# Dependent steps two k-tiles later, operand sums on VectorE, and another order of the last tokens' norm, in a two-layer decoder kernel

## The chip, the cores and the metric

The kernel runs on one core of a Trainium2 chip. The metric is the device time of one execution in microseconds (us), the median of several. TensorE is called PE, VectorE DVE, ScalarE ACT, GpSimd POOL, SyncE SP. Each engine works through its own queue in order, and waits on semaphores for what other engines produce.

## What is computed

Two decoder layers over 512 tokens of width 1024, all float32 at the interface. Each layer is `h = h + rmsnorm(mixer(rmsnorm(h)))`. Layer 0's mixer (differential attention beside a chunkwise matrix memory, then an output projection) is not touched. Layer 1's mixer, where nearly all of the change lies, is:

```python
def odd_mixer(h, sg_norm_g, w_in, w_spatial, b_spatial, w_out):
    p = jnp.einsum('bsd,de->bse', h, w_in)          # 512 x 1024 by 1024 x 6144
    u, v, z = _split(p, (2048, 2048, 2048))
    u = jax.nn.gelu(u)
    v = rmsnorm(jax.nn.gelu(v), sg_norm_g)
    vg = v.reshape(B, 4, 128, 8, 256)
    wm = w_spatial * causal                         # 8 groups of 128 x 128
    vs = jnp.einsum('gts,bcsgd->bctgd', wm, vg) + b_spatial.T[None, None, :, :, None]
    y = u * vs.reshape(B, S, 2048) * jax.nn.silu(z)
    return jnp.einsum('bse,ed->bsd', y, w_out)      # 512 x 2048 by 2048 x 1024
```

## The kernel before

**Precision.** A float32 matrix product is made from three matmuls: each operand is split into a high half (a rounding copy, on ACT) and a low half (the operand minus its high half, on DVE), and high by high, high by low and low by high are added in PSUM. The names `wh`, `wl` are the halves of weights, `A11s`, `S3s` and the like those of the activations.

**Groups.** Layer 1 is eight groups, 0 to 7. Each multiplies a 512 x 1024 activation block by a 1024 x 1024 weight block with seven half-size products in place of eight. A group is a row of seven phases, P1, P6, P2, P7, Q5, Q4, Q3 (group 0: P1, P2, P7, P6, Q5, Q4, Q3). A phase uses one activation operand (A11, S2, A12, S3, S1, A22, S4 in the usual order) and one weight operand. The S operands are sums of blocks of the activation; `U2` and the reloaded `B` blocks are sums of weight blocks, made partly by DVE (`sum2`) and partly by DMAs that add into their target (`add`, on POOL's queue). Groups 0 and 1 make v, groups 2 to 5 make u and z and multiply them into `y1T`, groups 6 and 7 are the output projection over the two halves of y. Groups 2 to 5 use 256-column matmuls, the others 512-column ones.

**The order of work is written out by hand.** In `Group.run` a phase is eight k-tiles: a k-tile is three matmuls of 512 columns (six of 256). After each k-tile `tick()` advances a counter and issues whatever `later(dt, fn)` has put at that count, so `later(2, f)` puts f's instructions into their engines' queues two k-tiles on. `need(n)` issues the weight splits (`Group.item`) ahead of use: item m holds a quarter of the weights of half a phase. When a half of a bank has its last k-tile (k-tile 6 or 8 of a phase), `hook(ph, q, o)` issues what reads the bank o: copies on ACT and sums on DVE which combine the seven products, and activation functions (`done`). Since queues are in order, an instruction that waits for another engine holds up all that stands behind it in its own queue.

**Hand-over.** The last projection of layer 0 ends with four token tiles (i = 0 to 3). For each, `f1` (L1214) squares the result on ACT (L325), takes the scale `pr` (L1217, DVE, then POOL), `residual` (L1223) adds into h1, `next_norm` squares again and takes `rs_b` (L95, then L96 on POOL), the product `xn_b` (L1203, DVE) follows, PE transposes it (L1136), and `blocks_of` makes the operands A11, A12 (tiles 0, 1) and S3, A22, S2 (tiles 2, 3). `R1`, `R2`, `R3` are k-tile delays in this chain; in the projection a k-tile is also three matmuls of 512 columns. S1 and S4 are sums over all tokens (`sum_split`, L1190).

**Operands of the last projection.** `prepare(c, ph, q, order)` runs during group 5 (c = 0) and group 6 (c = 1). After each phase it splits the operand that takes the slot just freed, in the order A11, A22, A12, S3, S2, S1, S4. The sums that S3, S2 and S1 need (A22 += A21, then A21 += A11, then A11 += A22) are three chained 512 KB DMAs on POOL's queue (L1333 to L1335), issued with the split of A22; the last (A12 = A11 - A12, L1329) is on DVE. The split of S3 is issued five eighths of the way through the group.

**Tail.** In group 7 each output token tile is finished by `value` (squares on ACT, gain on DVE or POOL) and `finish_token`: a sum and a scale on DVE, a power on POOL, two products on DVE (L1455) and two DMAs out. The four finishes stand one after the other in DVE's queue.

Of the kernel before, what the change touches and what calls it, by code (L numbers as in the profile page):

```python
# [41 lines left out]
R2 = (4, 4, 2, 4)  # L42
R3 = (4, 4, 5, 4)
# [13 lines left out]
def hybrid_kernel(tc, x, pre_g0, w_in0, b_ig, b_fg, conv_w, conv_b, lq1, lk1, lq2, lk2,  # L57
# [8 lines left out]
    with ExitStack() as ctx:  # L66
# [912 lines left out]
        def split_block(nm, src, n=0):  # L979

            d = SS[n][nm] = new_split(nm)
            nc.scalar.copy(d[:, 0], src)  # L982
            nc.vector.tensor_tensor(d[:, 1], src, d[:, 0], ALU.subtract)  # L983

        class Group:
# [31 lines left out]
            def item(self, m):  # L1017
# [15 lines left out]

# [13 lines left out]
            def run(self, kind, banks, hook):  # L1047
# [7 lines left out]
                for n, ph in enumerate(self.order):  # L1055
# [5 lines left out]
                    for q, pr in seq:  # L1061
                        need(self.base + 2 * (2 * n + pr + 3 + q) + 2)
# [32 lines left out]
        def combine(g, done):  # L1095

            s1, u2, u3 = new_su(g)

            def hook(ph, q, o):
                if ph == "P1":  # L1100
                    nc.scalar.copy(s1[:, q, :], o)
                elif ph == "P6":
                    if g > 0:
                        nc.vector.tensor_tensor(o, o, s1[:, q, :], ALU.add)
                    nc.scalar.copy(u2[:, q, :], o)
                    if g == 0:
                        b = banks[1][q]
                        nc.vector.tensor_tensor(b, b, u2[:, q, :], ALU.add)
                        nc.scalar.copy(u3[:, q, :], b)
                elif ph == "P2":  # L1110
                    if g == 0:
                        nc.vector.tensor_tensor(o, o, s1[:, q, :], ALU.add)
                    done("C11", q, o)
                elif ph == "P7":
                    if g > 0:
                        nc.scalar.copy(u3[:, q, :], o)
                elif ph == "Q5":
                    nc.vector.tensor_tensor(u3[:, q, :], o, u3[:, q, :], ALU.subtract)
                    done("C22", q, u3[:, q, :])
                elif ph == "Q4":  # L1120
                    done("C21", q, o)
                else:
                    nc.vector.tensor_tensor(u2[:, q, :], o, u2[:, q, :], ALU.subtract)
                    done("C12", q, u2[:, q, :])
            return hook
# [25 lines left out]
        def blocks_of(i, xn):  # L1151
# [14 lines left out]
            low = []  # L1166

            def f0():
                src = turned(i, xn, 0)
                nc.vector.tensor_tensor(s3, Af[0][:, :, t0], src, ALU.subtract)  # L1170
                low.append(split_high("S3", t, s3))

            def f1():
                src = turned(i, xn, 1)
                low.pop()()
                nc.vector.scalar_tensor_tensor(s2, s3, -1.0, src, ALU.mult, ALU.subtract)
                split_tile("A22", t, src)
                low.append(split_high("S2", t, s2))

            def f2():  # L1180
                low.pop()()
                if t == 1:
                    later(6, lambda: sum_split("S1", Af[0][:, :, 0:256], Af[1][:, :, 256:512]))
                    later(16, lambda: sum_split("S4", Af[1][:, :, 0:256], Af[1][:, :, 256:512]))
            later(R3[i], f0)
            later(R3[i] + 1, f1)
            later(R3[i] + 3, f2)

        def sum_split(nm, dst, b):
            nc.vector.tensor_tensor(dst, dst, b, ALU.add)  # L1190
            split_block(nm, dst)
# [22 lines left out]
        def f1(i, o):  # L1214
# [11 lines left out]
            later(R1, residual)  # L1226
# [64 lines left out]
        nc.vector.tensor_reduce(rv, sv, axis=AX.X, op=ALU.add)  # L1291
        rstd_of(rv, rv, 2048, 4)
# [4 lines left out]
        def mix(j, f):  # L1297
# [5 lines left out]
            if f == 0:  # L1303
                y1T.append(slot(YT[j], f"y1T{j}"))
            nc.vector.scalar_tensor_tensor(
                y1T[j][:, f, :].rearrange("p (c t) -> p c t", c=4),
                s[:].rearrange("p (c t) -> p c t", c=4), col(C_SG + 4 * j + f),
                sw["bsp"][:, g, :].unsqueeze(1).to_broadcast([P, 4, P]), ALU.mult, ALU.add)
# [5 lines left out]
        def prepare(c, ph, q, order):  # L1314
# [11 lines left out]

            def step():
                if nm == "S4":
                    nc.vector.tensor_tensor(A12, A11, A12, ALU.subtract)  # L1329
                ST[nm] = tag  # L1330
                split_block(nm, src[nm], c + 1)
                if nm == "A22":
                    nc.gpsimd.dma_start(A22, A21, accum_op=ALU.add)  # L1333
                    nc.gpsimd.dma_start(A21, A11, accum_op=ALU.add)
                    nc.gpsimd.dma_start(A11, A22, accum_op=ALU.add)  # L1335
            later(1, step)

        def uz_group(j):
# [3 lines left out]
            def times(c, q, o, fn):  # L1342
# [9 lines left out]
                if c == "C11":  # L1352
                    later(6 if j == 0 else 1, mul)
                else:
                    mul()

            def done(c, q, o):
# [6 lines left out]
                if c == "C21" and q == 1:  # L1364
                    nc.scalar.preload_act_table(AF.Silu)
                    for q_, o_ in wait:
                        times("C22", q_, o_, AF.Silu)
# [37 lines left out]
        def chunk0():  # L1405
# [3 lines left out]
            def hook(ph, q, o):  # L1409
                if ph == "P1":  # L1410
                    nc.scalar.copy(s1[:, q, :], o)
                elif ph == "P6":
                    nc.vector.tensor_tensor(o, s1[:, q, :], o, ALU.subtract)
                    nc.scalar.copy(u2[:, q, :], o)
# [22 lines left out]
        def chunk1():  # L1437
# [10 lines left out]
            def finish_token(t, q, y0_, y1_):  # L1448
                i = 2 * t + q
                rs = st(1, f"pr1{i}")  # L1450
                nc.vector.tensor_tensor(rs, sq[:, i, 0:1], sq[:, i, 1:2], ALU.add)
                rstd_of(rs, rs, D, 1)
# [71 lines left out]
```

## Time and profile before

| | us |
|---|---|
| time, median of 3 runs | 968.01 (967.96 to 968.61) |
| the profiled execution | 970.75 |
| its span, first to last instruction | 969.0 |
| PE busy in the span | 887.2 |
| DVE, ACT, POOL busy | 577.9, 485.1, 203.6 |
| mean granted PE clock, of full speed | 0.964 |

The span is cut into windows below; a pause of PE inside a window is the window's length less PE's busy time there. A row of a timeline gives in brackets how long the engine stood idle before the instruction and what released it. Ends of matmuls are modelled, so paces are taken from starts.

### The profile page before, as it was taken

The numbers are of one execution on the slowest core, as the hardware profiler recorded it, in microseconds if no ns is written. First come the engines' busy times: TensorE is split into PE (matmuls) and PEld (weight loads), VectorE is DVE, ScalarE is ACT, GpSimd is POOL, SyncE is SP. The second block draws the span as 40 slices with busy tenths as digits, with TensorE's granted clock in tenths as the row PEclk, the third lists the DMA queues.
The fourth block names the chain that finished last, engine by engine and source line by source line (L and its number), as shares of the span: only waits on it lengthen the run. The fifth ranks groups of instructions, "written<-read, shape, count | busy, mean of one in ns | idle before, by whom it ended". The sixth has DMA issues, their size and how long they took to land.

```text
span 969.0 us, 12665 instructions
## 1 busy us (share of the span) xinstructions
PE 887.2 (92%) x4739; PEld 751.6 (78%) x4739; DVE 577.9 (60%) x1026; ACT 485.1 (50%) x926; POOL 203.6 (21%) x276
## 2 busy tenths in 40 slices
PE   7999999999999999999999977998999999386592
PEld 5778888878888888788888755778999999364482
DVE  4467555657754766753431775666767675472675
ACT  5333433446665576654421645675665664352451
POOL 3210022502457135541100210111111011111211
PEclk8999999999999999999999989999999999699797
DMA  8232322312133222222527456676768676559542
GB/s 267 67 131 87 90 63 65 111 43 66 47 89 105 67 66 67 87 87 87 180 103 212 152 135 173 127 221 131 189 147 191 163 182 159 124 110 256 91 108 87
DMA packets 61379, 119.51 MB, mean 123 GB/s; under 512 B 4795, under 2 KB 7942, under 8 KB 61190
## 3 DMA queue, kind: packets, MB, share of 16 engines
q1 hardware_dynamic: 42822, 81.47, 26.1%
q0 software_dynamic: 17344, 34.09, 18.8%
q10 hardware_dynamic: 1152, 3.15, 0.9%
q8 instruction: 37, 0.61, 0.3%
q14 instruction: 24, 0.20, 0.1%
HBM read 111.35 MB, written 4.20 MB: 119 GB/s over the span
## 4 chain that ended last, share of the span: by engine, by line
PE 61%; DVE 13%; ACT 10%; DMA 8%; issue 6%; POOL 1%; SPq 0%; DVEq 0%; POOLq 0%; ACTq 0%
PE pj L275 40%; PE bank L1083 11%; DMA y1T<-y1T 5%; PE bank L1073 2%; PE ao L781 1%; ACT junk L325 1%; PE vs L1301 1%; DMA B<-in_l_w_out_dram 1%; DVE nm L750 1%; DVE U L1013 1%; DMA U<-in_l_w_in_dram 1%; ACT p L751 1%; DVE wlg5P L1024 1%; ACT wh L225 1%; PE sc L745 1%
## 5 line engine op out<-in xcount | busy, mean ns | idle before, releaser
L227 DVE TENSOR_TENSOR wl<-raw,wh 128x512 fp32r<-128x512 f32 x126 | 89.3, 726 | 106.4 <-ACT wh L225 106.0
L275 PE MATMUL pj<-wh,hT 128*128 128x512 f32 x320 | 129.0, 403 | 2.6 <-ACT hT L320 1.3
L275 PE MATMUL pj<-wl,hT 128*128 128x512 f32 x320 | 126.6, 396 | 0.0
L275 PE MATMUL pj<-wh,lT 128*128 128x512 f32 x320 | 126.3, 395 | 0.1
L225 ACT CAST wh<-raw 128x512 fp32r<-128x512 f32 x159 | 93.1, 613 | 40.7 <-DMA raw<-in_l_w_out_dram 19.1
L275 PE MATMUL pj<-hT,wh 128*128 128x512 f32 x192 | 77.8, 405 | 0.2 <-ACT mo L880 0.2
L275 PE MATMUL pj<-hT,wl 128*128 128x512 f32 x192 | 75.8, 395 | 0.0
L275 PE MATMUL pj<-lT,wh 128*128 128x512 f32 x192 | 75.8, 395 | 0.0
L275 PEld LDWEIGHTS pj<-wh,hT 128*128 128x128 f32 x320 | 60.6, 189 | 14.8 <-ACT mz L897 1.7
L275 PEld LDWEIGHTS pj<-wh,lT 128*128 128x128 f32 x320 | 60.5, 189 | 14.1 <-DVE lT L321 0.4
L227 POOL TENSOR_TENSOR wl<-raw,wh 128x512 fp32r<-128x512 f32 x34 | 45.4, 1338 | 119.2 <-ACT wh L225 116.6
L275 PEld LDWEIGHTS pj<-wl,hT 128*128 128x128 f32 x320 | 60.7, 190 | 11.7 <-DVE wl L227 0.4
L751 ACT ACTIVATE p<-sc,nm 128x512 f32<-128x512 f32 (+3 forms) x64 | 33.8, 528 | 47.2 <-DVE nm L750 45.7
L1006 POOL DMA_DIRECT2D B<-in_l_w_in_dram x12 | 15.5, 1292 | 197.9 <-DMA B<-in_l_w_in_dram 54.0
L275 PE MATMUL pj<-wh,yh 128*128 128x512 f32 x128 | 51.2, 400 | 0.0
L275 PE MATMUL pj<-wh,yl 128*128 128x512 f32 x128 | 50.6, 395 | 0.0
L275 PE MATMUL pj<-wl,yh 128*128 128x512 f32 x128 | 50.3, 393 | 0.0
L275 PEld LDWEIGHTS pj<-hT,wl 128*128 128x128 f32 x192 | 36.0, 188 | 8.8
L275 PEld LDWEIGHTS pj<-hT,wh 128*128 128x128 f32 x192 | 36.0, 188 | 8.7 <-ACT mo L880 0.6
L275 PEld LDWEIGHTS pj<-lT,wh 128*128 128x128 f32 x192 | 36.1, 188 | 7.9
L750 DVE TENSOR_REDUCE nm<-sc 128x1 f32<-128x512 f32 (+3 forms) x64 | 31.4, 491 | 2.2
L983 DVE TENSOR_TENSOR S3s<-y1T,S3s 128x1024 fp32r<-128x1024 f32 x2 | 2.5, 1226 | 43.5 <-ACT S3s L982 43.5
(628 smaller groups left out, 2293.3 us busy)
## 6 DMA issues: line engine op xcount, KB each, us to landing
raw<-in_l_w_in_dram SPq DMA_DIRECT2D x64, 512.0 KB, 3.6
B<-in_l_w_in_dram SPq DMA_DIRECT2D x24, 1024.0 KB, 7.7
B<-in_l_w_in_dram POOLq DMA_DIRECT2D x12, 1024.0 KB, 9.2
raw<-in_l_w_out_dram SPq DMA_DIRECT2D x16, 512.0 KB, 4.0
B<-in_l_w_out_dram SPq DMA_DIRECT2D x8, 1024.0 KB, 12.0
U<-in_l_w_in_dram POOLq DMA_DIRECT2D x6, 1024.0 KB, 8.5
B<-in_l_w_out_dram POOLq DMA_DIRECT2D x4, 1024.0 KB, 11.1
y1T<-y1T POOLq DMA_DIRECT2D x6, 512.0 KB, 5.4
```

The lines of the kernel that those rows point to most:

```text
L225: nc.scalar.copy(wh, raw[:, n % 2, :])
L227: eng.tensor_tensor(wl, raw[:, n % 2, :], wh, ALU.subtract)
L275: nc.tensor.matmul(self.outs[i], lhsT=a, rhs=b, start=(n == 0 and m == 0), stop=(n == len(self.ks) - 1 and m == ms[-1]))
L325: nc.scalar.activation(junk[:, :n], src, AF.Square, accum_out=dst)
L745: nc.tensor.matmul(s[:, :n2], lhsT=qs, rhs=dk[p][c][:, h, 0:n2], start=True, stop=False)
L750: nc.vector.reduce_max(nmx[:, c:c + 1], s[:, :nk], axis=AX.X, negate=True)
L751: nc.scalar.activation(pr[:, c, :nk], s[:, :nk], AF.Exp, bias=nmx[:, c:c + 1], accum_out=sm[:, c:c + 1])
L781: nc.tensor.matmul(o[:, i * P:(i + 1) * P], lhsT=aT[:, kb * P:(kb + 1) * P], rhs=dv[p][:, kb, h * P:(h + 1) * P], start=(kb == 0), stop=(k ...
L1006: nc.gpsimd.dma_start(self.X[dst], self.block(nm), accum_op=ALU.add)
L1013: nc.vector.tensor_tensor(at("U2"), at("B11"), at("B12" if self.g else "B22"), ALU.add)
L1073: nc.tensor.matmul(o, lhsT=l, rhs=r, start=(start and k == 0 and m == 0), stop=(k == 3 and m == 2), skip_group_check=True)
L1083: nc.tensor.matmul(o[:, f * 256:(f + 1) * 256], lhsT=l, rhs=r, start=(start and k == 0 and m == 0 and f == 0), stop=(k == 3 and m == 2), s ...
```

## The change

Nearly every step of layer 1 that reads another engine's result is issued two k-tiles after the one that makes it: the low half of a weight pair after its high half, the low half of an operand after its high half, bank copies after bank sums, products after activation functions. The loads and adding DMAs that a freed weight block allows move with the low halves, two k-tiles. The three chained adding DMAs in `prepare` become DVE sums behind the low halves of A22, A12 and S3, and the sum for S4 moves behind the low half of S1. At the hand-over `residual` comes two k-tiles after `f1` instead of three, tile 3's product comes two k-tiles and its operands four k-tiles earlier, tile 2's operands one later; S1 is summed in the same k-tile as tile 3's last operand and is ready some 10 k-tiles earlier. In group 0 the splits for phases three ahead come two k-tiles later. The norm of v moves from the end of group 1 into group 2 (k-tile 4). In the tail the scale and the products of a token tile are issued two k-tiles apart (tokens of the second half) or one (first half), interleaved with the next tile's steps.

```diff
-R2 = (4, 4, 2, 4)
-R3 = (4, 4, 5, 4)
+R2 = (4, 4, 3, 3)
+R3 = (4, 4, 6, 2)
...
-        def split_block(nm, src, n=0):
+        def split_block(nm, src, n=0, then=()):
             d = SS[n][nm] = new_split(nm)
             nc.scalar.copy(d[:, 0], src)
-            nc.vector.tensor_tensor(d[:, 1], src, d[:, 0], ALU.subtract)
+            def low():
+                nc.vector.tensor_tensor(d[:, 1], src, d[:, 0], ALU.subtract)
+                for f in then:
+                    f()
+            later(2, low)
...
                 wh, wl = self.W[ph, pr] = new_pair(f"g{self.g}{ph}{pr}")
-                nc.scalar.copy(wh, src)
-                nc.vector.tensor_tensor(wl, src, wh, ALU.subtract)
-                if ph == "P1" and self.g > 0:
-                    self.sum2(pr)
-                if pr == 0:
-                    return
+                def high():
+                    nc.scalar.copy(wh, src)
+                    later(2, low)
+                def low():
+                    nc.vector.tensor_tensor(wl, src, wh, ALU.subtract)
+                    if ph == "P1" and self.g > 0:
+                        self.sum2(pr)
+                    if pr == 1:
+                        self.freed(ph)
+                if ph == "P6" and self.g == 0:
+                    later(1, high)
+                else:
+                    high()
+            def freed(self, ph):
...
-                        need(self.base + 2 * (2 * n + pr + 3 + q) + 2)
+                        need(self.base + 2 * (2 * n + pr + 3 + (q if self.g or n > 1 else 0)) + 2)
...
-                    if g > 0:
-                        nc.vector.tensor_tensor(o, o, s1[:, q, :], ALU.add)
-                    nc.scalar.copy(u2[:, q, :], o)
-                    if g == 0:
-                        b = banks[1][q]
-                        nc.vector.tensor_tensor(b, b, u2[:, q, :], ALU.add)
-                        nc.scalar.copy(u3[:, q, :], b)
+                elif ph == "P6" and g > 0:
+                    tt(o, o, s1q, ALU.add)
+                    later(2, lambda: copy(u2q, o))
+                elif ph == "P6":
+                    copy(u2q, o)
+                    b = banks[1][q]
+                    later(2, lambda: tt(b, b, u2q, ALU.add))
+                    later(4, lambda: copy(u3q, b))
...
-            later(R3[i], f0)
-            later(R3[i] + 1, f1)
-            later(R3[i] + 3, f2)
+            for n, f in enumerate((f0, f1, f2, f3)):
+                later(R3[i] + 2 * n, f)
...
-            later(R1, residual)
+            later(2, residual)
...
+            then = dict(A22=tt(A22, A22, A21, ALU.add), A12=tt(A21, A21, A11, ALU.add),
+                        S3=tt(A11, A11, A22, ALU.add), S1=tt(A12, A11, A12, ALU.subtract))
             def step():
-                if nm == "S4":
-                    nc.vector.tensor_tensor(A12, A11, A12, ALU.subtract)
                 ST[nm] = tag
-                split_block(nm, src[nm], c + 1)
-                if nm == "A22":
-                    nc.gpsimd.dma_start(A22, A21, accum_op=ALU.add)
-                    nc.gpsimd.dma_start(A21, A11, accum_op=ALU.add)
-                    nc.gpsimd.dma_start(A11, A22, accum_op=ALU.add)
+                split_block(nm, src[nm], c + 1, [then[nm]] if nm in then else ())
             later(1, step)
...
-                if c == "C11":
-                    later(6 if j == 0 else 1, mul)
-                else:
-                    mul()
+                later(2, mul)
...
-            for i in range(4 if j == 0 else 0):
-                v = v1[0][:, i, :]
-                nc.vector.tensor_scalar(v, v, rv[:, i:i + 1], None, ALU.mult)
+            if j == 0:
+                later(4, v_norm)
...
-            def finish_token(t, q, y0_, y1_):
+            def finish_token(t, q, y0_, y1_, dt=2):
...
+                later(dt, norm)
+                later(2 * dt, store)
```

Where a line of a hook is left out above, its DVE sum or ACT copy stays and what reads it moves into `later(2, ...)`.

## Rows read from the trace of the kernel before

**Rows 1.** Page: PE's busy tenths in 40 slices; DMA issues (count, size, us to landing).

```profile
PE   7999999999999999999999977998999999386592
...
B<-in_l_w_out_dram SPq DMA_DIRECT2D x8, 1024.0 KB, 12.0
...
B<-in_l_w_out_dram POOLq DMA_DIRECT2D x4, 1024.0 KB, 11.1
```

**Rows 2.** Windows of the span: us, busy us of each engine (instructions), granted clock, DMA.

```profile
563.00:600.00 37.00, 25.10 (x96) 19.37 (x97) 23.39 (x27) 18.95 (x29) 3.12 (x3) 0.86 0.65 161
600.00:652.80 52.80, 50.33 (x218) 39.95 (x219) 31.73 (x32) 36.24 (x61) 8.11 (x8) 1.00 0.68 176
652.80:668.00 15.20, 12.64 (x93) 12.21 (x92) 10.16 (x15) 7.45 (x12) 3.61 (x3) 0.89 0.80 139
668.00:824.40 156.40, 156.40 (x1334) 156.39 (x1333) 106.34 (x118) 89.86 (x116) 14.05 (x11) 1.00 0.69 168
824.40:847.20 22.80, 8.07 (x50) 7.90 (x49) 9.80 (x10) 8.78 (x10) 2.54 (x2) 0.63 0.58 123
847.20:913.20 66.00, 42.72 (x170) 33.34 (x169) 34.99 (x36) 28.57 (x36) 8.21 (x7) 0.84 0.70 159
913.20:951.90 38.70, 38.70 (x169) 31.37 (x168) 30.21 (x35) 16.59 (x25) 8.32 (x7) 1.00 0.40 82
951.90:969.00 17.10, 0.03 (x1) 0.00 (x0) 9.19 (x19) 2.16 (x6) 1.62 (x3) 0.65 0.33 123
```

**Rows 3.** PE's timeline at its longer pauses: start, us, instruction, [idle before <- releaser].

```profile
568.15 1.08 PE L1136 MATMUL xnT<-ident,xn_b 128*128 128x128 f32 x4 [6.41 <-DVE xn_b L1203]
...
599.83 0.50 PE L1073 MATMUL bank<-whg0Q,A22s 128*128 128x512 f32 x1 [3.10 <-ACT u L1109]
...
663.34 2.05 PE L1301 MATMUL vs<-wmT,v 128*128 128x128 f32 x8 [2.51 <-DVE v L1372]
...
839.33 0.77 PE L1083 MATMUL bank<-S4s,whg5Q 128*128 128x256 f32 x2 [14.73 <-DVE u L1118]
...
906.32 0.77 PE L1073 MATMUL bank<-whg6Q,S4s 128*128 128x512 f32 x1 [18.99 <-DVE ca L1397]
```

**Rows 4.** Timelines of POOL, ACT and DVE around the pause at 824 us.

```profile
811.13 1.83 POOL L1333 DMA_DIRECT2D y1T<-y1T  x1
...
835.55 1.26 POOL L1335 DMA_DIRECT2D y1T<-y1T  x1 [4.58 <-DMA y1T<-y1T]
...
835.15 1.04 ACT L982 CAST S3s<-y1T 128x1024 fp32r<-128x1024 f32 x1 [20.91 <-DMA y1T<-y1T]
...
836.22 1.23 DVE L983 TENSOR_TENSOR S3s<-y1T,S3s 128x1024 fp32r<-128x1024 f32 x1 [20.43 <-ACT S3s L982]
837.37 1.22 DVE L1024 TENSOR_TENSOR wlg5Q<-B,whg5Q 128x1024 fp32r<-128x1024 f32 x1
```

**Rows 5.** DVE's timeline: a sum of two 128x1024 blocks of y1T.

```profile
858.55 1.22 DVE L1329 TENSOR_TENSOR y1T<-y1T,y1T 128x1024 f32<-128x1024 f32 x1
```

**Rows 6.** DVE's timeline at the hand-over: last token tile's scale and its product.

```profile
556.04 0.21 DVE L1217 TENSOR_SCALAR pr<-sp 128x1 f32<-128x1 f32 x1
...
567.26 1.41 DVE L1203 SCALAR_TENSOR_TENSOR xn_b<-h1b,rs_b,gains 128x512 f32<-128x512 f32 x2
```

**Rows 7.** POOL and ACT in group 0: the sum into U, and the bank copies after it.

```profile
580.79 1.28 POOL L1006 DMA_DIRECT2D U<-in_l_w_in_dram  x1 [7.01 <-issue]
...
589.34 1.04 ACT L1023 CAST whg0Q<-U 128x1024 fp32r<-128x1024 f32 x1 [1.13 <-DMA U<-in_l_w_in_dram]
...
599.19 0.59 ACT L1109 COPY u<-bank 128x512 f32<-128x512 f32 x1 [1.41 <-DVE bank L1108]
```

**Rows 8.** DVE's timeline in the tail: first and last token tile.

```profile
947.14 0.67 DVE L1476 TENSOR_TENSOR cb<-cb,bank 128x512 f32<-128x512 f32 x1
...
961.15 0.68 DVE L1397 SCALAR_TENSOR_TENSOR u<-bank,u 128x512 f32<-128x512 f32 x1
...
964.95 0.75 DVE L1455 SCALAR_TENSOR_TENSOR h1n<-u,pr,h1n 128x512 f32<-128x512 f32 x1
```

More of the change, by code (lines that the diff above doesn't have):

```diff
@@ L1290, in hybrid_kernel, with v_norm, scale @@
         v_group(1)
-        nc.vector.tensor_reduce(rv, sv, axis=AX.X, op=ALU.add)
-        rstd_of(rv, rv, 2048, 4)
+        def v_norm():
+            nc.vector.tensor_reduce(rv, sv, axis=AX.X, op=ALU.add)
+            rstd_of(rv, rv, 2048, 4)
+            def scale():
+                for i in range(4):
+                    v = v1[0][:, i, :]
+                    nc.vector.tensor_scalar(v, v, rv[:, i:i + 1], None, ALU.mult)
+            later(2, scale)
         y1T = []
@@ L1413, in hook @@
                     nc.vector.tensor_tensor(o, s1[:, q, :], o, ALU.subtract)
-                    nc.scalar.copy(u2[:, q, :], o)
+                    later(2, lambda: nc.scalar.copy(u2[:, q, :], o))
                 elif ph == "P2":
@@ L1446, in value, with norm, store @@
                 mul.tensor_tensor(y, y, gb1[:, n * 512:(n + 1) * 512], ALU.mult)
-            def finish_token(t, q, y0_, y1_):
+            def finish_token(t, q, y0_, y1_, dt=2):
                 i = 2 * t + q
                 rs = st(1, f"pr1{i}")
-                nc.vector.tensor_tensor(rs, sq[:, i, 0:1], sq[:, i, 1:2], ALU.add)
-                rstd_of(rs, rs, D, 1)
-                for hf, y in ((0, y0_), (1, y1_)):
-                    h = h1n[t][:, 2 * q + hf, :]
-                    nc.vector.scalar_tensor_tensor(h, y, rs, h, ALU.mult, ALU.add)
-                    (nc.sync, nc.scalar)[hf].dma_start(out[i * P:(i + 1) * P, hf * 512:hf * 512 + 512], h)
+                def norm():
+                    nc.vector.tensor_tensor(rs, sq[:, i, 0:1], sq[:, i, 1:2], ALU.add)
+                    rstd_of(rs, rs, D, 1)
+                def store():
+                    for hf, y in ((0, y0_), (1, y1_)):
+                        h = h1n[t][:, 2 * q + hf, :]
+                        nc.vector.scalar_tensor_tensor(h, y, rs, h, ALU.mult, ALU.add)
+                        (nc.sync, nc.scalar)[hf].dma_start(
+                            out[i * P:(i + 1) * P, hf * 512:hf * 512 + 512], h)
+                later(dt, norm)
+                later(2 * dt, store)
             def hook(ph, q, o):
@@ L1466, in hook @@
                     nc.vector.tensor_tensor(y, y, o, ALU.add)
-                    value("C11", q, y, nc.gpsimd)
+                    later(2, lambda: value("C11", q, y, nc.gpsimd))
                 elif ph == "P7":
@@ L1472, in hook @@
                     minus(y, o, y)
-                    value("C22", q, y, nc.gpsimd)
+                    later(2, lambda: value("C22", q, y, nc.gpsimd))
                 elif ph == "Q4":
@@ L1482, in hook @@
                     value("C12", q, y, nc.vector)
[L1483 removed]
+                    finish_token(0, q, ca_of("C11", q), y, 1)
             later(26, lambda: load_back(1))
@@ L1489, in hybrid_kernel @@
         chunk1()
+        while clock["due"]:
+            tick()
 _INS = ['x', 'l0_pre_g', 'l0_w_in', 'l0_b_igate', 'l0_b_fgate', 'l0_conv_w', 'l0_conv_b',
```

67 lines of the change are left out of this document (35 added, 32 removed).

## Prediction, made before the result was known

> **What bounds the kernel now.** I read the page's slices first: PE is nine tenths busy almost everywhere, and the exceptions are a dip at slices 23 and 24, deep holes from slice 34 to 37 and the last slice [rows 1]. The windows put numbers on them [rows 2]. From 668 to 824.4 us PE is never idle: no step moved there can gain anything, it can only lose. The holes are four.
>
> The *hand-over and group 0* (563 to 600): PE is busy 25.1 of 37.0 us. Its timeline names the longest pauses, 6.41 us for tile 3's product and 3.10 us for a bank copy on ACT [rows 3]. *Groups 0 to 2* (600 to 668): 2.5 and 2.6 us idle, the latter one pause of 2.51 us for v times its norm, after which the clock is low (0.89 granted over the window). *Groups 5 and 6* (824.4 to 913.2): pauses of 14.73 and 18.99 us [rows 3]. *The tail*: PE is done at 951.9, the span ends at 969.0.
>
> For the big pauses the page names a DVE instruction as the releaser, but that is only the last link. POOL issues the first chained DMA at 811.13 and the third at 835.55; ACT's split of S3 has stood 20.91 us waiting for a y1T DMA, DVE's low half of S3 20.43 us for ACT, and the low halves of the weights that PE needs stand behind it, from 837.37 [rows 4]. So an operand needed only in group 6 stops group 5.
>
> **Groups 5 and 6: the chained DMAs go.** Three adds of 128x1024 per chunk move to DVE. A sum of that shape on y1T takes 1.22 us [rows 5], with about 1.15 from start to start [rows 4], so 3.5 us per chunk, 7 in all, in place of DMA chains whose first and third members are issued 24.4 us apart. Each sum is issued six k-tiles before the split that needs it. What remains is PE's own work. In 913.2 to 951.9 the 168 matmuls of group 7 take 38.7 us without a pause, 0.230 us each; group 6 has as many, 38.7. Group 5's last phase is 48 matmuls of half the columns, 5.6 us. Now 824.4 to 913.2 takes 88.8 us, half-clock stretches after the pauses included (granted 0.63 and 0.84 in the two windows); 88.8 - 38.7 - 5.6 = 44.5 us. I take 44, leaving half a microsecond for small waits. The y1T DMAs also leave POOL's queue and the DMA engines to the weights.
>
> **The two-k-tile delays there.** A low half of weights is issued about 14 k-tiles before use and would be at 12, that is 8.3 us at three matmuls of 0.230 us; it takes 1.22 us. The loads and adding DMAs behind it start 1.4 us later. They take 11 to 12 us for these weights [rows 1] and the sum into U is issued 26 k-tiles, 18 us, before its split: hidden, and if that cover went it would cost the 1.4 us once per group. Bank copies move from 11 to 9 k-tiles ahead of the next matmul on that bank: 6.2 us for a copy of 0.59 us [rows 7]. Cost zero, gain zero in the stretch where PE is full. What the delays do change is that DVE and ACT stop waiting for each other in turn.
>
> **The hand-over.** DVE takes tile 3's scale at 556.04 and starts its product at 567.26 [rows 6]: 11.2 us, because tile 2's operands stand in between. In the new order there stand between scale and product: a gain (0.7), two low halves of weights (2.4), the residual (two products, 1.4), the norm's scale (0.15), a difference and a low half of tile 2 (1.4), 6.1 us, and DVE waits some 1.2 us for ACT's pass over 128x1024 (1.04 in [rows 4]). 7.3 in place of 11.2, and the scale itself some 0.7 earlier: product at about 562.6, 4.6 us earlier. PE meets it four k-tiles (2.8 us) earlier in its own work, so the pause stays about 5.6 us and the gain is 1.9. S1, now ready 10 k-tiles earlier, no longer stops phase Q5.
>
> The next limit is U. Its adding DMA is issued at 580.79, ACT splits the result at 589.34, the last bank copy behind it is at 599.19 and PE goes on at 599.83 [rows 7, 3]. Walking the new queues I get the DMA at about 578.5, landing 8.5 us later at 587.0; then on ACT and DVE in turn a high half (1.04), its low half (1.22), the sum for S4 (1.22), its copy (1.04), two bank copies (1.2), a high half (1.04) and the last bank copy (0.6): 594.4, against 599.83. PE has by then waited some 5 us, and a spell of half clock afterwards, as after the longer pauses now [rows 3], takes 0.7 back. Ahead by 4.7 us. Then the 2.5 us of 600 to 652.8 and the 2.6 us of the mix pause with about 1 us of low clock behind it should go: v's sums end about 3 k-tiles into group 2, the norm and scale need some 3 us more and the mix is 11 k-tiles (7.6 us) in. Together 4.7 + 2.5 + 2.6 + 1.0 = 10.8, call it 11. Bounds: 4 if only the later small pauses go; 23 if every idle microsecond from 563 to 668 (11.9 + 2.5 + 2.6) and some 6 us of low clock go.
>
> **The tail.** One token tile takes 961.15 to 965.70, 4.55 us on DVE with its waits for ACT and POOL; four in a row start at 947.14, 4.8 us before PE ends [rows 8]. In the new order the first half's steps are two k-tiles apart. Tile one can start when its bank is done, 10 k-tiles (6.9 us) before PE's end; DVE's own work per tile is 3.1 us, and the second tile's waits are filled by the first's steps, so two tiles take 7.7 us. The last two still run 4.5 each, as the second's difference stands behind the first's products. End of the last product: -6.9 + 7.7 + 9.1 = 9.9 us after PE, against 13.8 now; the DMA out and the end behind it are the same 3.3. Gain 4; bounds 2 and 5.
>
> **Sum.** 44 + 11 + 4 = 59 us. The profiled execution took 970.75 (span 969.0, 1.75 outside it), so 911.75 for one like it; the median lies 2.74 lower at 968.01: **909.0**. About 0.2% is what a measurement of this kernel can tell from no change.
>
> **Rivals.**
>
> *DVE becomes the bound in groups 5 and 6.* In group 5 it would have 26 instructions of 128x1024 (fourteen low halves of weights, six of operands, two sums into U, four sums of y1T) and 18 of half that, 26 x 1.15 + 18 x 0.65 = 41.6 us, where PE needs 38.7 us and four mixes, 64 matmuls of 128 columns, 3.7. In group 6: 27 x 1.15 + 6 x 0.65 = 35 of 38.7. From 668 to 824.4 DVE is busy 106 of 156 us, so there is no such load to look at now. If a fifth of its time still goes in waits, it falls 9.6 us behind in group 5 and 5 in group 6, of which the 8.3 us of lead cover the first: 6 to 15 us lost, 915 to 924. It decides once DVE is over 8.3 us behind. For it: phases Q5 to Q3 of group 5 ask 20 us of DVE (13 x 1.15 + 8 x 0.65) where PE's 144 matmuls of 256 columns take 16.6. Against it: the waits are what the delays remove, and group 6 leaves time to catch up.
>
> The Trainium skill speaks against the sums' new place: "Perfetto Trace Analysis", section "Optimizing Scalar/DVE Operations", says that a saturated DVE should have work moved off it, and here work is moved onto it. By that rule the time would be that of this rival, 915 to 924; the trace so far shows DVE at 68% where PE is full, which leaves room [rows 2].
>
> *The hand-over is no faster.* Tile 3's product is still late and U with it, since DVE's work there is the same and only its order changes; then only the later small pauses and low clock go, 6 in place of 11, or 4 at the least: 914 to 916.
>
> *The hand-over's pauses go almost entirely*, if DVE is less behind than I walk it: 12 us more, 897.
>
> *The delays reach PE.* If DVE is more than 12 k-tiles behind throughout, each of the 112 weight pairs arrives two k-tiles (1.4 us) late: up to 155 us. It is slower than before once 43 of the pairs pay. In the full stretch they have 12 k-tiles of lead, so it is unlikely; at its full price the time would be about 1064.
>
> *The change doesn't do what it says*: the sums on DVE wait so long behind other work that S3 is as late as now. Then 968. S3's sum would have to be 20 us late.
>
> **How the numbers follow.** The forecast, 903 to 914: 0.56. DVE as the bound: 0.17. Hand-over no faster: 0.10. Hand-over much faster: 0.11. Delays reach PE: 0.03. As late as before: 0.03. So faster 0.95, same 0.02, slower 0.03. The range takes in the DVE rival and most of the better hand-over: 898 to 923.
>
> **What would show it.** Right: no pause of PE over 2 us from 600 us on; no y1T DMA on POOL; the stretch from the start of group 5's last phase to group 7 in about 45 us; the product of tile 3 near 562.6 and one pause there of 5 to 6 us, another of about 5 before phase Q4 of group 0; DVE over 85% busy in groups 5 and 6; the tail near 13 us. Wrong: PE waiting for low halves of weights in groups 5 to 6 (DVE rival), PE waiting on banks in 668 to 824 (delays too long), a U that lands as late as 589, or a pause before the first mix.

## The result and the profile after

The changed kernel takes 911.5 us (median of four runs, 909.9 to 912.2) beside 968.2 us for the kernel before on the same chip: a ratio of 0.9412, with a 95% interval of 0.9396 to 0.9428. The forecast was 909.0 with a range of 898 to 923. The profiled execution has a span of 908.2 us, against 969.0; the two profiled executions, of 970.75 and 909.89 us, lie 60.9 us apart, the medians 56.7.

Windows of the changed kernel, cut where the places of [rows 2] now lie (columns as there):

```profile
549.20:605.70 56.50, 45.76 (x187) 36.79 (x186) 43.71 (x52) 35.57 (x56) 6.69 (x7) 0.88 0.59 149
605.70:645.10 39.40, 39.40 (x177) 32.32 (x176) 24.11 (x25) 27.30 (x45) 9.07 (x8) 1.00 0.83 214
645.10:773.90 128.80, 128.80 (x1105) 128.76 (x1104) 91.37 (x106) 79.30 (x105) 12.51 (x10) 1.00 0.70 173
773.90:817.15 43.25, 43.25 (x370) 43.25 (x369) 39.13 (x43) 29.35 (x36) 3.81 (x3) 1.00 0.69 171
817.15:855.70 38.55, 38.55 (x171) 31.57 (x170) 37.09 (x38) 27.20 (x34) 4.39 (x4) 1.00 0.89 231
855.70:894.60 38.90, 38.90 (x169) 31.42 (x167) 27.46 (x36) 16.54 (x25) 7.83 (x7) 1.00 0.41 89
894.60:908.20 13.60, 0.10 (x1) 0.00 (x0) 7.16 (x14) 1.45 (x4) 1.08 (x2) 0.63 0.36 133
```

From 605.7 us to its end PE does not stand still for as much as 0.25 us. Groups 5 and 6 (773.90 to 855.70) keep DVE busy for 39.13 of 43.25 and 37.09 of 38.55 us, 90 and 96%, and PE still never waits for it. From 540 us on its timeline has two longer pauses, both in group 0:

```profile
562.22 1.09 PE L1154 MATMUL xnT<-ident,xn_b 128*128 128x128 f32 x4 [5.70 <-DVE xn_b L1222]
...
591.82 0.79 PE L1089 MATMUL bank<-whg0Q,A22s 128*128 128x512 f32 x1 [5.04 <-ACT u L1127]
```

The rows of DVE, POOL and ACT that answer to [rows 6, 7] are these: tile 3's product at 561.33 in place of 567.26, the DMA that adds into U at 577.09 in place of 580.79, ACT's split of the result at 586.27 in place of 589.34, and the bank copy that PE waits for at 591.17 in place of 599.19 (here it is the first of the two copies behind U, there the second). Some 1.6 us of each difference lies ahead of group 0, as the table below shows.

```profile
561.33 1.41 DVE L1222 SCALAR_TENSOR_TENSOR xn_b<-h1b,rs_b,gains 128x512 f32<-128x512 f32 x2
...
577.09 1.28 POOL L1011 DMA_DIRECT2D U<-in_l_w_in_dram  x1 [4.46 <-DVE wlg0P L1034]
...
586.27 1.05 ACT L1030 CAST whg0Q<-U 128x1024 fp32r<-128x1024 f32 x1 [7.59 <-DMA U<-in_l_w_in_dram]
...
591.17 0.59 ACT L1127 COPY u<-bank 128x512 f32<-128x512 f32 x1
```

To see where the time went in this and the later kernels, four stretches are cut in each kernel's PE timeline at the same matmuls: the first of group 0 on A11, the first of group 5 on A22 (the phase before the one that stood 14.73 us in [rows 3]), the first of group 7 on A11, the last of all, and the end of the span. The head is what lies ahead of the first.

| us | head | group 0 to 5 (A22) | rest of 5, and 6 | group 7 | tail | span |
|---|---|---|---|---|---|---|
| before | 550.83 | 267.95 | 94.46 | 38.30 | 17.46 | 969.0 |
| after | 549.27 | 256.58 | 49.84 | 38.62 | 13.89 | 908.2 |
| 1: sums only | 551.24 | 267.96 | 55.94 | 38.51 | 17.75 | 931.4 |
| 2: all but the sums | 549.58 | 256.52 | 84.38 | 38.31 | 13.91 | 942.7 |
| 3: new order only | 550.07 | 269.47 | 95.03 | 38.29 | 16.44 | 969.3 |
| 4: tail only | 550.46 | 267.52 | 94.19 | 38.62 | 13.91 | 964.7 |
| 5: all but the delays | 549.32 | 270.47 | 54.81 | 39.28 | 13.82 | 927.7 |
| 6: more DVE work | 550.32 | 256.94 | 55.38 | 42.50 | 13.86 | 919.0 |
| 7: tile 3 later | 550.36 | 252.64 | 49.85 | 38.62 | 13.83 | 905.3 |
| 8: Q3 before Q4 | 550.27 | 253.18 | 49.85 | 38.62 | 13.88 | 905.8 |
| 9: 7 and 8 | 550.36 | 250.96 | 49.85 | 38.62 | 13.91 | 903.7 |
| 10: low halves later still | 550.72 | 256.45 | 51.99 | 38.41 | 13.83 | 911.4 |
| 11: all but the new order | 549.52 | 254.54 | 49.85 | 38.62 | 13.87 | 906.4 |
| 12: only half of the delays | 549.52 | 263.94 | 53.46 | 39.65 | 13.83 | 920.4 |

The span lost 60.8 us: 1.6 in the head, 11.4 up to group 5, 44.6 in the rest of group 5 and group 6, 3.6 in the tail, and 0.3 given back in group 7. The head scatters by 2 us over kernels that share its code, so that 1.6 is not counted for the change. The table is of one execution each. Of the 11.4 us up to group 5, cut again at the first matmul on A11 of each group, 3.9 are in group 0 (60.3 us before, 56.4 after), 2.3 in group 1 (41.7 and 39.5) and 5.2 in group 2 (47.7 and 42.5).

### The profile page after: what moved, and what is told of

Read it like the earlier page. It is cut to its first block, busy times and chain, and to the rows that moved or that the text cites. A ratio compares the mean times of both kernels' runs of the same rounds, so it can differ in the third digit from the quotient of the medians.

```text
span 908.2 us, 12659 instructions
## 1 busy us (share of the span) xinstructions
PE 877.0 (97%) x4739; PEld 746.2 (82%) x4739; DVE 581.6 (64%) x1032; ACT 487.5 (54%) x926; POOL 196.7 (22%) x270
## 4 chain that ended last, share of the span: by engine, by line
PE 83%; DVE 6%; ACT 5%; issue 3%; DMA 2%; POOL 1%; SPq 0%; DVEq 0%; POOLq 0%; ACTq 0%
PE pj L275 42%; PE bank L1099 17%; PE bank L1089 14%; PE vs L1328 2%; PE ao L781 2%; DVE nm L750 1%; DMA U<-in_l_w_in_dram 1%; ACT p L751 1%; ACT junk L325 1%; ACT wh L225 1%; PE sc L745 1%; DMA x<-in_x_dram 1%; PE yT L852 1%; PE mN L653 1%; PE sc L747 1%
## 5 line engine op out<-in xcount | busy, mean ns | idle before, releaser
L275 PEld LDWEIGHTS pj<-wl,hT 128*128 128x128 f32 x320 | 60.3, 189 | 11.4 <-DVE wl L227 0.2
L275 PEld LDWEIGHTS pj<-wh,yl 128*128 128x128 f32 x128 | 24.0, 188 | 5.4
## 6 DMA issues: line engine op xcount, KB each, us to landing
B<-in_l_w_out_dram POOLq DMA_DIRECT2D x4, 1024.0 KB, 10.2
```

Of the source, the lines that this page charges most:

```text
L275: nc.tensor.matmul(self.outs[i], lhsT=a, rhs=b, start=(n == 0 and m == 0), stop=(n == len(self.ks) - 1 and m == ms[-1]))
```

## The experiments

**1. The sums on DVE alone**, in the kernel before.

```diff
 split_block(nm, src[nm], c + 1)
-if nm == "A22":
-    nc.gpsimd.dma_start(A22, A21, accum_op=ALU.add)
-    nc.gpsimd.dma_start(A21, A11, accum_op=ALU.add)
-    nc.gpsimd.dma_start(A11, A22, accum_op=ALU.add)
+add = {"A22": (A22, A21), "A12": (A21, A11), "S3": (A11, A22)}.get(nm)
+if add:
+    nc.vector.tensor_tensor(add[0], add[0], add[1], ALU.add)
```

> The kernel before with one part alone: the three chained adds of y1T blocks are DVE sums behind the low halves of A22, A12 and S3; nothing is moved by two k-tiles. My theory (the parts add up, the DMA chain alone made both big pauses): 44 us less, 924, both pauses gone, group 0 and the tail as before. Rival (the sums need the delays): DVE and ACT, waiting for each other in turn, can't carry the sums, PE waits for low halves in groups 5 and 6: 930 to 940.

Measured: 932.3 us, ratio 0.9618 [0.9600, 0.9637], some 37 us less than before, and in the table 38.5 us from group 5 on, against 44.6 in the full change. The time lies in the rival's range, not at the theory's 924: the chained DMAs are the greater part, but not the 44 that the prediction gave them. In place of the two deep holes PE now has four small pauses in group 6, of which these are the longest:

```profile
839.28 0.50 PE L1073 MATMUL bank<-whg6P,S2s 128*128 128x512 f32 x1 [1.75 <-DVE u L1123]
...
853.87 0.50 PE L1073 MATMUL bank<-whg6P,S3s 128*128 128x512 f32 x1 [1.55 <-ACT u L1413]
```

**2. The change with its sums put back on the chained DMAs.**

```diff
-then = dict(A22=tt(A22, A22, A21, ALU.add), A12=tt(A21, A21, A11, ALU.add),
-            S3=tt(A11, A11, A22, ALU.add), S1=tt(A12, A11, A12, ALU.subtract))
+dma = lambda d, a: (lambda: nc.gpsimd.dma_start(d, a, accum_op=ALU.add))
+then = dict(A22=[dma(A22, A21), dma(A21, A11), dma(A11, A22)],
+            S1=[tt(A12, A11, A12, ALU.subtract)])
```

> The changed kernel with one part undone: the three adds are chained DMAs on POOL's queue again, issued behind the low half of A22; all delays, the hand-over and the tail stay. My theory: both pauses are back at 15 and 19 us with their half-clock spells, 44 us more, 955. Rival (the delays carry part of those 44, since the split of S3 no longer stands ahead of so much): 925 to 945.

Measured: 944.4 us, ratio 0.9739 [0.9719, 0.9759]. The sums are worth 33 us on top of the rest, and the rest without them 25: the rival's time, not the theory's 955. In groups 5 and 6 the rest shortens the holes even with the DMAs there, from 94.46 to 84.38 us. POOL still issues the chain's first and third member 23.5 us apart (24.4 in [rows 4]), and PE stands for their end:

```profile
795.17 1.83 POOL L1355 DMA_DIRECT2D y1T<-y1T  x1
...
818.63 1.26 POOL L1355 DMA_DIRECT2D y1T<-y1T  x1 [5.98 <-DMA y1T<-y1T]
```

```profile
822.40 0.77 PE L1099 MATMUL bank<-S4s,whg5Q 128*128 128x256 f32 x2 [10.49 <-DVE u L1136]
...
882.32 0.77 PE L1089 MATMUL bank<-whg6Q,S4s 128*128 128x512 f32 x1 [16.71 <-DVE ca L1419]
```

**3. The new order at the hand-over alone**, in the kernel before: the new places of the tiles' norms and splits, the residual and the first needs of group 0, without a delay anywhere else (but for S1 and S4, which are split two k-tiles after their sums).

```diff
-R2 = (4, 4, 2, 4)
-R3 = (4, 4, 5, 4)
+R2 = (4, 4, 3, 3)
+R3 = (4, 4, 6, 2)
...
-later(R1, residual)
+later(2, residual)
```

> The kernel before with the hand-over's order alone (residual at two k-tiles, tile 3's product and operands earlier, S1 summed with its last operand, group 0's splits a little later). My theory: the pause for tile 3's product shrinks by 2 us net, the 3 us for S1 go, the pause for the bank copy behind U moves but stays: 5 to 6 us less, 962 to 963. Rival (the order is worth nothing without the delays, DVE's work is the same): 966 to 968.

Measured: 969.05 us beside 969.05, ratio 0.9998 [0.9988, 1.0007]: nothing, so the theory of 5 to 6 us falls. PE meets tile 3's product 4.33 us earlier (563.82, against 568.15 in [rows 3]; 0.76 of this is a shorter head) and the wait for S1 is gone, but U's chain ends where it ended: the second wait for ACT's copies is over at 599.21, against 599.83.

```profile
563.82 1.09 PE L1136 MATMUL xnT<-ident,xn_b 128*128 128x128 f32 x4 [6.26 <-DVE xn_b L1204]
...
599.21 0.50 PE L1073 MATMUL bank<-whg0Q,A22s 128*128 128x512 f32 x1 [1.64 <-ACT u L1109]
```

**4. The tail alone**, in the kernel before: the new `chunk1` (group 7's hook, `finish_token` and the final loop of ticks).

```diff
+later(dt, norm)
+later(2 * dt, store)
...
+while clock["due"]:
+    tick()
```

> The kernel before with the last group's hooks and the interleaved finish of the token tiles alone. My theory: the tail shrinks from 17.1 to about 13.6 us after PE's end, 3.4 us less: 964.8. Rival (DVE is still behind when the tail begins, because the low halves before it wait for ACT in turn, so the first tile can't start ten k-tiles before PE's end): 966 to 967.

Measured: 966.4 us beside 968.4, ratio 0.9976 [0.9967, 0.9986]: 1.4 to 3.2 us. The table's tail shrinks from 17.46 to 13.91 us, as much as in the full change; the time shows a little less than this 3.55, as the rival had it (966 to 967).

**5. The change without the two-k-tile delays** in groups 0 to 6: low halves, bank copies, elementwise steps and mixes are issued at once, as before. Order, sums, tail and the new place of v's norm are those of the change, and so are the delays of the splits of S1 and S4 and of the scaling of v.

```diff
-later(2, low)
+low()
...
-later(2, lambda: copy(u2q, o))
+copy(u2q, o)
...
-later(2, mul)
+if c == "C11":
+    later(6 if j == 0 else 1, mul)
+else:
+    mul()
```

> The changed kernel with the two-k-tile delays of groups 0 to 6 taken back (low halves, bank copies, products and activations issued at once again); sums on DVE, hand-over, v's norm and tail stay. My theory: where PE is full the delays are worth nothing, in groups 0 to 2 some 4 to 7 us, and some waits of DVE for ACT come back in groups 5 and 6 without reaching PE: 915 to 919. Rival (the delays are what lets DVE carry the sums): PE pauses in groups 5 and 6, 922 to 935. Second rival (they are worth nothing anywhere): 911 to 912.

Measured: 930.8 us, ratio 0.9602 [0.9586, 0.9619], in the first rival's range and far from the theory's 915 to 919. Beside the rest of the change the delays are worth 19 us: 13.9 up to group 5, where without them nothing at all is left of the gain (270.47 us, against 267.95 before), and 5.0 in groups 5 and 6. ACT's timeline without them, and then that of the change, at the split of U's first sum:

```profile
575.93 0.60 ACT L1302 ACTIVATE v<-bank 128x512 f32<-128x512 f32 x1 [0.98 <-DVE bank L1131]
...
578.13 1.04 ACT L1030 CAST whg0P<-U 128x1024 fp32r<-128x1024 f32 x1
```

```profile
574.49 1.05 ACT L1030 CAST whg0P<-U 128x1024 fp32r<-128x1024 f32 x1 [1.87 <-PE bank L1089]
575.44 0.59 ACT L1302 ACTIVATE v<-bank 128x512 f32<-128x512 f32 x1
```

Without the delay, ACT stands at v's activation until DVE has added to the bank, and the split that leads to U's DMA is behind it. With the delay, the activation comes after the split, and has nothing to wait for by then (the split's own wait is for the sum into U, which DVE ends at 574.40, though the row names PE). That is the smaller part of the 3.64 us by which the split comes later. The larger is DVE's: its sum into U, which the split reads, ends 2.6 us later, behind waits of DVE for ACT's splits. DVE's timeline without the delays, and then that of the change:

```profile
571.73 1.23 DVE L1034 TENSOR_TENSOR wlg0P<-U,whg0P 128x1024 fp32r<-128x1024 f32 x1 [1.03 <-ACT whg0P L1030]
...
575.80 1.22 DVE L1018 TENSOR_TENSOR U<-B,B 128x1024 f32<-128x1024 f32 x1
```

```profile
573.19 1.21 DVE L1018 TENSOR_TENSOR U<-B,B 128x1024 f32<-128x1024 f32 x1
```

At the start of group 6 the two engines hand each other each of these steps. Timeline without the delays:

```profile
837.53 0.63 ACT L1370 ACTIVATE sz3C<-u 128x512 f32<-128x512 f32 x1 [3.27 <-DVE u L1141]
...
838.19 0.69 DVE L1374 SCALAR_TENSOR_TENSOR y1T<-sz3C,y1T 128x512 f32<-128x512 f32 x1 [0.76 <-ACT sz3C L1370]
```

The same step in the change waits for nothing on DVE, whose queue is full of other work meanwhile:

```profile
819.52 0.64 ACT L1370 ACTIVATE sz3C<-u 128x512 f32<-128x512 f32 x1 [1.90 <-DVE u L1141]
819.94 1.22 DVE L1034 TENSOR_TENSOR wlg6P<-U,whg6P 128x1024 fp32r<-128x1024 f32 x1
...
821.68 0.68 DVE L1374 SCALAR_TENSOR_TENSOR y1T<-sz3C,y1T 128x512 f32<-128x512 f32 x1
```

The Trainium skill says in "PSUM — Partial Sum Buffer", section "Engine vs sequencer instructions", that the queues of ScalarE and VectorE are strictly first in, first out. These rows agree: a step that waits 0.76 us holds everything behind it.

**6. More DVE work in the change**: in groups 5 and 6 the low halves of the operands are written twice, 14 instructions of 128x1024 more.

```diff
-nc.vector.tensor_tensor(d[:, 1], src, d[:, 0], ALU.subtract)
+for _ in range(2 if n else 1):
+    nc.vector.tensor_tensor(d[:, 1], src, d[:, 0], ALU.subtract)
```

> The changed kernel with seven more DVE instructions of 128x1024 in each of groups 5 and 6: the low halves of the last projection's operands are written twice (same values). 8 us of DVE work per group, 16 in all. My theory (DVE has some slack and 8 us of lead): the work no longer fits into group 5, DVE falls 8 to 10 us behind, PE loses 2 to 9 us: 913 to 920. Rival (DVE is already the bound there): all 16 us show, 927.

Measured: 920.0 us, ratio 0.9499 [0.9486, 0.9512], 8.5 us more than the change for some 16 us of work (14 x 1.15). That is in the theory's range. The window of group 6 has DVE busy for 43.80 of 44.07 us; PE pauses there for 3.4 us in four places, and behind it, in group 7, for 2.40:

```profile
818.57:862.64 44.07, 40.52 (x171) 30.93 (x169) 43.80 (x44) 26.18 (x33) 4.40 (x4) 1.00 0.75 193
```

```profile
870.70 0.47 PE L1090 MATMUL bank<-whg7P,S2s 128*128 128x512 f32 x1 [2.40 <-DVE cb L1419]
```

So the limit that the DVE rival spoke of is real; by an estimate (16 us added, 8.5 of them lost) some 8 us of added work lie between it and the change.

**7. Tile 3's operand steps six k-tiles later**, in the change.

```diff
-R3 = (4, 4, 6, 2)
+R3 = (4, 4, 6, 8)
```

> The changed kernel with tile 3's transposes and operands six k-tiles later (R3 of tile 3: 8 for 2). My theory: the 5.7 us pause is where PE's in-order queue meets the transposes before the product is there; six k-tiles of phase P2 put ahead of them cover 4.1 us of it, and with a short pause the clock stays up, but U's chain behind it moves little, so the pause before phase Q4 grows by part of it: 906 to 909. Rival 1 (it all comes back before Q4, as U's chain is the limit): 911. Rival 2 (S3 or S1 come too late): 912 or more.

Measured: 908.8 us, ratio 0.9389 [0.9374, 0.9403]. Up to group 5 it takes 3.9 us less than the change. The wait for tile 3's product falls from 5.70 to 1.58 us, the waits for its operands come up in its place (1.92 and 2.09), and the one for U falls from 5.04 to 1.49. The time is the theory's, the way is not: the pause before Q4 was to grow. U lands no earlier (ACT splits it at 586.58, against 586.27), but the sum for S4 and its split, six k-tiles later too, no longer stand ahead of the bank copy that PE waits for, which comes at 589.53 in place of 591.17.

```profile
563.30 0.63 PE L1154 MATMUL xnT<-ident,xn_b 128*128 128x128 f32 x4 [1.58 <-DVE xn_b L1222]
569.79 0.51 PE L1089 MATMUL bank<-whg0P,S3s 128*128 128x512 f32 x1 [1.92 <-ACT S3s L1163]
572.61 1.22 PE L1089 MATMUL bank<-whg0P,S3s 128*128 128x512 f32 x2 [2.09 <-DVE S3s L1164]
590.17 0.50 PE L1089 MATMUL bank<-whg0Q,A22s 128*128 128x512 f32 x1 [1.49 <-ACT u L1127]
```

**8. Phases Q3 and Q4 of group 0 exchanged**, in the change, so that the phase that needs U's last copies comes last.

```diff
-ORDER0 = ("P1", "P2", "P7", "P6", "Q5", "Q4", "Q3")
+ORDER0 = ("P1", "P2", "P7", "P6", "Q5", "Q3", "Q4")
...
-(q if self.g or n > 1 else 0)
+(q if self.g or n in (2, 3) else 0)
```

> The changed kernel with phases Q3 and Q4 of group 0 exchanged, so that the block U, which a DMA still adds into, is needed eight k-tiles (5.5 us) later. My theory: the 5.0 us pause before Q4 is only the wait for U's landing and the copies behind it, and goes with its spell of half clock: 904 to 906. Rival (ACT and DVE stop at the split of U all the same, and hold the sum S4 and the bank copies): the pause moves to Q3, 910 to 912.

Measured: 907.5 us, ratio 0.9368 [0.9355, 0.9381]. This lies between the theory and the rival: the pause of 5.04 us does not go, but becomes one of 2.86 before Q3, for another step:

```profile
590.42 0.47 PE L1089 MATMUL bank<-whg0Q,S4s 128*128 128x512 f32 x1 [2.86 <-DVE u L1136]
```

**9. Both**, and the sum for S4 six k-tiles sooner (`later(14, ...)` becomes `later(8, ...)`).

> The changed kernel with tile 3's operand steps six k-tiles later, phases Q3 and Q4 of group 0 exchanged, and the sum for S4 six k-tiles sooner. Theory: the two pauses that are left at the hand-over are one shortage of DVE time seen twice; the late turn of tile 3 alone left pauses of 1.58, 1.92 and 2.09 us there, as much as the 5.70 us that it removed, and what it gained came from U (1.49 us in place of 5.04). The exchange can then take only that last 1.49 us: 906 to 908. Rival: the two gains add up, 911.5 - 2.7 - 4.0 = 905 or less.

Measured: 906.3 us beside 970.2, ratio 0.9339 [0.9319, 0.9359], the fastest of all. The table has 250.96 us up to group 5, 1.7 less than 7 alone, which is what the theory said; the ratios (0.5% below 7, with intervals of 0.2%) would allow the rival's sum too. PE's pauses are those of 7, with 1.35 us for S4's bank in place of 1.49 for U.

**10. Low halves of the weights later still**, in the change, from group 2 on.

```diff
-later(2, low)
+later(6 if self.g > 1 else 2, low)
```

> The changed kernel with the low halves of the weights issued six k-tiles after the high halves from group 2 on, in place of two. Theory (the prediction's lead of 12 k-tiles): 8 k-tiles, 5.5 us, are still left for an instruction of 1.22 us, so nothing changes: 910 to 913. Rival: in groups 5 and 6 DVE is 90 to 96% busy and runs several k-tiles behind its queue's plan, so that the later halves reach PE: 916 to 930.

Measured: 912.6 us beside 970.2, ratio 0.9405 [0.9384, 0.9426]: no change that the time can show. The trace shows a little: 2.1 us more in groups 5 and 6, with two pauses for low halves (0.85 and 0.46 us), which by the lead of 8 k-tiles should not be there. Rows of PE, ACT and DVE:

```profile
825.24 0.50 PE L1089 MATMUL bank<-wlg6P,S2s 128*128 128x512 f32 x1 [0.85 <-DVE wlg6P L1034]
```

```profile
812.24 1.05 ACT L1030 CAST whg6P<-B 128x1024 fp32r<-128x1024 f32 x1 [3.81 <-DMA B<-in_l_w_out_dram]
```

```profile
813.32 1.23 DVE L1034 TENSOR_TENSOR wlg6P<-B,whg6P 128x1024 fp32r<-128x1024 f32 x1 [2.02 <-ACT whg6P L1030]
```

The edit moves more than the low halves: the loads behind them go four k-tiles later as well. Here ACT waits 3.81 us for group 6's first weights and DVE 2.02 us for ACT, where the change splits the same weights at 807.00 without a wait. So the late low halves can come from late weights as well as from a DVE that is behind its queue's plan, and the run does not part the two.

**11. The change with the old order at the hand-over**: delays, sums and tail stay.

```diff
-R2 = (4, 4, 3, 3)
-R3 = (4, 4, 6, 2)
+R2 = (4, 4, 2, 4)
+R3 = (4, 4, 5, 4)
...
-later(2, residual)
+later(R1, residual)
```

> The changed kernel with the old order at the hand-over (tiles' norms, differences and sums where they stood before), and with all the delays and the sums on DVE. Theory: order and delays are worth something only together; tile 3's product is again near 567 us and stops phase P2 and what is queued behind it, so U's chain starts late: 919 to 923. Rival: the delays alone bring U forward, and the order is worth nothing even beside them: 910 to 914.

One delay at the hand-over stays, that of the splits of S1 and S4 behind their sums.

Measured: 908.1 us beside 970.2, ratio 0.9360 [0.9341, 0.9378]. The rival holds, and more than holds: the old order is no slower beside the delays, if anything 0.5% faster. Tile 3's product is 4.3 us later than in the change and stops PE for 6.17 us; the wait for S1 is back; U's DMA is issued only 1.4 us later, and the waits for its copies are 1.45 and 0.72 us in place of 5.04.

```profile
565.64 1.41 DVE L1221 SCALAR_TENSOR_TENSOR xn_b<-h1b,rs_b,gains 128x512 f32<-128x512 f32 x2
...
566.53 1.09 PE L1154 MATMUL xnT<-ident,xn_b 128*128 128x128 f32 x4 [6.17 <-DVE xn_b L1221]
...
578.47 1.28 POOL L1011 DMA_DIRECT2D U<-in_l_w_in_dram  x1 [5.75 <-issue]
...
583.62 0.50 PE L1089 MATMUL bank<-whg0Q,S1s 128*128 128x512 f32 x1 [1.65 <-ACT S1s L982]
...
591.62 0.50 PE L1089 MATMUL bank<-whg0Q,A22s 128*128 128x512 f32 x1 [1.45 <-ACT u L1127]
594.00 0.50 PE L1089 MATMUL bank<-whg0Q,A22s 128*128 128x512 f32 x1 [0.72 <-ACT u L1127]
```

Behind U's landing ACT goes from the split of U to the second bank copy. Its waits for DVE on that way, before (from 589.34 to 599.19, the last wait being that of [rows 7]), in the change (from 586.27), and in this run:

```profile
592.28 0.59 ACT L1109 COPY u<-bank 128x512 f32<-128x512 f32 x1 [1.42 <-DVE bank L1108]
...
596.25 1.05 ACT L982 CAST S4s<-Af 128x1024 fp32r<-128x1024 f32 x1 [2.43 <-DVE Af L1190]
```

```profile
589.75 1.04 ACT L982 CAST S4s<-Af 128x1024 fp32r<-128x1024 f32 x1 [1.00 <-DVE Af L1209]
...
593.22 0.59 ACT L1127 COPY u<-bank 128x512 f32<-128x512 f32 x1 [0.52 <-DVE bank L1126]
```

```profile
586.90 1.05 ACT L1030 CAST whg0Q<-U 128x1024 fp32r<-128x1024 f32 x1 [3.33 <-DMA U<-in_l_w_in_dram]
...
590.99 0.59 ACT L1127 COPY u<-bank 128x512 f32<-128x512 f32 x1 [1.12 <-DVE bank L1126]
...
593.36 0.59 ACT L1127 COPY u<-bank 128x512 f32<-128x512 f32 x1
```

The way takes 9.85 us before, 6.95 in the change and 6.46 here, with 5.26, 1.52 and 1.12 us of waits for DVE in it.

**12. Half of the delays**: as 5, but with the low halves of weights and operands still two k-tiles late. Only the delays of bank copies, elementwise steps and mixes are undone.

> The changed kernel with the delays of the bank copies, the elementwise steps and the mixes undone in groups 0 to 6, and the low halves of weights and operands still two k-tiles late. Theory: what costs time is an engine that stands at the head of its queue for a bank step of the other, so nearly all of the 19 us that came back without any delay come back here too: 924 to 931. Rival: it is the low halves, three quarters of DVE's time there, that have to be late: 911 to 917.

Measured: 922.5 us beside 970.2, ratio 0.9509 [0.9484, 0.9534], between the theory and the rival. By the table the late low halves bring 6.5 us up to group 5 and 1.4 after it (12 against 5), the late bank steps 7.4 and 3.6 (the change against 12). Both kinds count, the bank steps somewhat more.

## Why the prediction was right, and where its steps were not

The time was right, and by places so was the sum: 44 for groups 5 and 6 measured 44.6, 11 for the hand-over and the groups behind it 11.4, 4 for the tail 3.6. The places add up to 59.3 us with group 7, where the medians are 56.7 apart: the profiled execution before was 2.7 us above its median, the one after 1.6 below. What the steps said of the cause was right only in part.

*The chained DMAs.* That they were the real link behind DVE's name in the chain of waits is shown by 1 and 2, from both sides. The term of 44 was mis-sized as theirs: alone they bring 38.5 in that place. The other 5 to 6 come from the delays, since without these a group 6 with the sums on DVE has pauses of its own (1, 5).

*The two-k-tile delays: the step that failed.* "Cost zero, gain zero in the stretch where PE is full" is true there: from the first matmul of group 3 to the phase on A22 in group 5 it takes 118.26 us both before and after. But the prediction gave the delays no term anywhere, and spoke of the two engines' turns only in a sentence beside the sum. Beside the rest of the change they are worth 19 us in time, 13.9 of them in groups 0 to 2, and the rows of 5 and 11 show the engines' waits for each other as what they change.

*The hand-over: right size, wrong owner.* By the sum's own terms, which the groups match roughly, group 0 was to gain 4.7 us and gained 3.9, group 1 2.5 and gained 2.3, group 2 3.6 and gained 5.2. The walk met the rows of DVE and POOL: product 561.33 (562.6 forecast), U's DMA 577.09 (578.5), its landing 586.27 (587.0). But 1.6 us of this is the shorter head: counted from group 0's first matmul, U lands 1.5 us earlier than before, where the walk had 2.3. That PE's two waits met the forecast is luck. The 5.6 us for the first (measured 5.70) does not follow from the working, where 6.41 less a gain of 1.9 is 4.5; PE came to the transposes 3.7 us earlier in place of 2.8, so that the pause shrank by 0.7 only. The second (5.04, forecast 5) is for the first bank copy behind U, at 591.17, where the walk has PE go on after the last, at 594.4.

And the walk went through the new queues with order and delays in them together, and named the order as the part. Experiment 3 has the order without the delays and gains nothing; 11 has the delays without the order and gains everything. What the delays bring there is that ACT and DVE stand less at the head of their queues for each other: 3.74 us less of such waits behind U's landing in the change, 4.14 in 11, while the landing itself comes only 1.5 and 1.1 us earlier. It is not the earlier tile 3. Of the small later pauses, the one before the mix stays in 5 (4.58 us, with v's norm in its new place) and is gone in the change, so the new place alone does not remove it.

*DVE as the bound* did not come true, at 90 and 96% busy; 6 shows that it would have with some 8 us more of work (an estimate, see there). The Trainium skill says in "Perfetto Trace Analysis", section "Optimizing Scalar/DVE Operations", that moving work off a saturated DVE may make sense; this bears on 6, and not yet on the change. How much of the 12 k-tiles of lead that the prediction reckoned with is used up stays open: in 10, where 8 were left, PE waited 0.85 and 0.46 us, but the weights came late there too.

*The tail.* The last product of the change starts at 904.09 and ends 10.2 us after PE's end of 894.6; 9.9 were forecast. Of this gain 3.55 us show in the trace of 4, and 1.4 to 3.2 in its time.

Two things stay open. One is why the old order is slightly faster beside the delays: the low clock after the single pause of 5.04 us (below) would cover it, 2.4 us by the windows where the table has 2.0 between the two, but no run changed the clock alone. The other is what v's norm adds by its new place: no run has it in the old place beside the delays.

## What to carry to other kernels

Where two in-order engines hand results to each other, look at what stands behind each waiting step, even where neither engine is two thirds busy (63 and 51% in the first window of [rows 2]): issuing the dependent step a little later, behind work that is ready, brought 19 us here and let DVE run at 96% without stopping PE. When several parts of a change meet in one place, a walk through the final queues gives the time but not the part that earned it; undo one part at a time before keeping it. The order at the hand-over could be left out, and 9 shows that what follows from the pauses left in the profile is worth 0.8% more than the change, though only 0.2%, no more than the interval, beside 11, which simply leaves the order out.

## What the runs showed of the hardware

Behind the pause of 5.04 us the clock costs more than the 0.7 us that the prediction allowed. Windows of the change from the end of its pause of 5.04 us to group 1, and of experiment 11 over the same work, which had waits of 1.45 and 0.72 us there:

```profile
591.82:605.67 13.85, 13.85 (x48) 11.10 (x49) 11.46 (x13) 11.73 (x20) 1.27 (x1) 0.79 0.45 153
```

```profile
591.62:603.81 12.19, 11.46 (x49) 9.05 (x49) 9.79 (x11) 11.03 (x19) 0.00 (x0) 1.00 0.49 173
```

The granted clock is 0.79 in the one, part of it at 1.2 GHz and part at 2.4, and 1.00, all at 2.4 GHz, in the other, and the same matmuls take 13.85 us of PE's time against 11.46: 2.4 us lost behind the one long pause, none behind the two short ones. In experiment 7 short pauses came with a fall too: in the window behind the first of its three (1.58, 1.92 and 2.09 us in 11 us), which holds the other two, the granted clock is 0.77.

```profile
564.47:577.04 12.57, 8.56 (x29) 6.19 (x28) 12.21 (x16) 9.91 (x15) 2.57 (x2) 0.77 0.52 125
```
